# First feed-forward block of a streaming encoder layer: plain products for the first two gated tiles, and the second projection taken product by product per token pair, summed in PSUM

## The chip, the cores and the metric

One NeuronCore of a Trainium2 chip runs one launch of the kernel. The engines in the text are TensorE (PE, matrix products), VectorE (DVE), ScalarE (ACT), GpSimd (POOL) and SyncE (SP), whose queue issues the DMA transfers. The metric is device time in microseconds; less is better.

## The reference

One layer of an encoder: a SwiGLU feed-forward half-step, a mixing step with gated linear attention and stick-breaking attention, and a second SwiGLU half-step, each followed by a layer norm. Tokens are 1024 of a new stream and 64 of a running one, 1088 in all. Only the first half-step is touched:

```python
D_MODEL = 1024; D_FF = 2816; DN_ALPHA = 2 ** 0.25

def swiglu(x, w_in, w_out):
    gate, up = jnp.split(x @ w_in, 2, axis=-1)
    return (jax.nn.silu(gate) * up) @ w_out

def encoder_layer(x, ...):
    h = layer_norm(DN_ALPHA * x + 0.5 * swiglu(x, ffn1_w_in, ffn1_w_out), ln1_g, ln1_b)
    mix, s_new, k_new, v_new = token_mix(h, ...)
    h = layer_norm(DN_ALPHA * h + mix, ln2_g, ln2_b)
    return layer_norm(DN_ALPHA * h + 0.5 * swiglu(h, ffn2_w_in, ffn2_w_out), ln3_g, ln3_b), ...
```

## The kernel before

All data are kept with features on the 128 partitions and tokens along the free dimension. Operands of TensorE are fp32r. To keep fp32 accuracy each operand is split into a high part (`wh`, `xh`: a rounded copy made by ACT) and a low part (`wl`, `xl`: source minus high part, made by POOL or DVE), and one product is three matmuls: wh·xh, wh·xl, wl·xh.

The first half-step has two stages. Stage 1 makes the gate and up projections and the gated product: 22 tiles of 128 hidden features. Stage 2 is the second projection, from 2816 hidden features to 1024. Both use a scheme of seven products in place of eight for 2x2 blocks: input features in two halves, output features in two halves (gate and up in stage 1), tokens in four quarters of 272. Two quarters make a token pair, c = 0 or 1, with 544 tokens. Seven combinations of the input blocks (`xc0` to `xc6`) meet seven combinations of the weight blocks (`weight_forms`, sums `sm`), and the sums of the products are made partly in PSUM, partly by DVE and ACT.

Stage 1. `make_x` builds the seven input forms of each token pair from loaded tiles `big`. The first two tiles (`FIRST`) are taken for token pair 0 first and then for token pair 1, the other 20 for both pairs together: 168 matmuls of 128x272 to a tile, 84 when one pair is done. `gate_up` evicts each product for each pair by itself, 272 columns wide. After every second tile `hidden_forms` makes the seven forms of two hidden tiles and stores them in DRAM, one tensor `d_hc` to a pair of hidden tiles; SP issues those stores.

Stage 2. Six `GROUPS` of hidden pairs (one of 1 pair, five of 2) are run over one after the other; the `xc` slots of stage 1 take the hidden forms that `load_group` reads back, and `load_out` brings the weights in tiles `raw`. The output is a sum in SBUF, `acc` (1024 x 1088), which begins as x (four loads at the line with `acc<-x`). `out_tile` computes the seven products of a group, and DVE adds each of them into `acc` (`onto`) once it is done. The layer norm of tokens 0 to 543 is woven between the last four output tiles of token pair 1. Then the stage's pools close, `split1` splits the normed tokens for the next stage, the first input weights of that stage are loaded (`raw<-w_in`), and `low_rank` and the value projections follow.

The tile framework puts the instructions of each engine in a fixed order when the kernel is built and sets the semaphores; an engine runs its own list in that order. `ahead(gen, n)` makes weight forms n products early.

Of the kernel before, what the change touches and what calls it, by code (L numbers as in the profile page):

```python
# [21 lines left out]
P = 128  # L22
# [12 lines left out]
HW = 272  # L35
NP = NH // 2
GROUPS = [(0, 1), (1, 2), (3, 2), (5, 2), (7, 2), (9, 2)]
# [54 lines left out]
def tile_encoder_layer(  # L92
# [21 lines left out]
    d_hc = [dr.tile([P, 7, 2, 2, HW], F32, name=f"d_hc{p}") for p in range(NP)]  # L114
# [9 lines left out]
    temps = [None, None]  # L124

    def tmp(w, tag):
        pool, bufs = temps
        t = pool.tile([P, 384], F32, name=tag, tag=tag, bufs=bufs[tag])
        return t[:, :w]
# [330 lines left out]

    def weight_forms(A, n, pool, on_pool):


        def form(src, i):
            wh = pool.tile([P, 4, P], F32R, name="wh", tag="wh", bufs=7)[:, :n, :]
            wl = pool.tile([P, 4, P], F32R, name="wl", tag="wl", bufs=7)[:, :n, :]
            nc.scalar.copy(wh, src)  # L467
            eng = nc.gpsimd if i in on_pool else nc.vector
            eng.tensor_tensor(wl, src, f32(wh), op=ALU.subtract)  # L469
            return wh, wl  # L470

        def add(a, b):
            t = pool.tile([P, 4, P], F32, name="sm", tag="sm", bufs=3)[:, :n, :]
            nc.vector.tensor_tensor(t, a, b, op=ALU.add)
            return t

        a11, a12, a21, a22 = A
        yield form(a11, 0)
        yield form(a12, 1)
        s1 = add(a21, a22)  # L480
        s2 = add(a11, s1)
        yield form(s2, 2)
        yield form(s1, 3)
        yield form(add(a11, a21), 4)
        yield form(a22, 5)
        yield form(add(a12, s2), 6)

    def token_forms(B, form, neg, add, sub):

        b11, b12, b21, b22 = B  # L490
        form(0, b11)
        form(1, b21)
        n1 = sub(b11, b12)
        t2 = add(b22, n1)
        neg(2, t2)
        form(3, n1)
        form(4, sub(b22, b12))
        form(5, sub(t2, b21))
        form(6, b22)

    def seven(forms, xs, cs, A, B, evac, want=None):

        n = None
        for i in range(NPROD):
            wh, wl = next(forms)
            bank = A if i in (0, 2, 4, 5) else B(i)
            fresh = i in (0, 1, 3)
            for c in cs:
                x = xs(i, c)
                n = len(x)  # L510
                for k, (xh, xl) in enumerate(x):
                    o = bank[:, c, :HW]
                    kw = dict(skip_group_check=True)
                    nc.tensor.matmul(o, wh[:, k, :], xh, start=(fresh and k == 0), stop=False, **kw)  # L514
                    nc.tensor.matmul(o, wh[:, k, :], xl, start=False, stop=False, **kw)  # L515
                    nc.tensor.matmul(o, wl[:, k, :], xh, start=False, stop=(k == n - 1), **kw)  # L516
            for c in cs:
                evac(i, c, bank[:, c, :HW])
            yield cost(3 * n * len(cs), HW)
# [6 lines left out]
    XF = [xa, xb]  # L526

    def bank_a():
        return pq.tile([P, 2, 512], F32, name="qa", tag="qa")

    def banks_b():
        held = {}

        def b(i):
            if i != 6:
                held[0] = pq.tile([P, 2, 512], F32, name="qb", tag="qb", bufs=2)
            return held[0]

        return b

    def big(dtype=F32):
        return p1.tile([P, 4 * HW], dtype, name="big", tag="big", bufs=6)

    def load_gate_up(j):
        raws = []
        for g in range(2):
            raw = ws.tile([P, 1024], F32, name="raw", tag="raw", bufs=4)
            r0 = (2 * j + g) * P
            nc.sync.dma_start(out=raw, in_=f1_in[r0 : r0 + P, :])
            raws.append(raw.rearrange("p (k m) -> p k m", m=P))  # L550
        g, u = raws
        return [g[:, :4], g[:, 4:], u[:, :4], u[:, 4:]]


    XC = {}

    def load_x(c):
        B = {}
        for jt in ((0, 0), (1, 0), (0, 1), (1, 1)):
            j, t = jt  # L560
            q = big()
            t0 = (2 * c + t) * HW
            nc.sync.dma_start(
                out=q.rearrange("p (k w) -> p k w", w=HW),
                in_=x[j * 512 : (j + 1) * 512, t0 : t0 + HW].rearrange("(k p) w -> p k w", p=P),
            )
            B[jt] = q
            yield q
        yield B

    def make_x(c, B, eng):
        XC[c] = [None] * NPROD

        def out(i):
            t = XF[c].tile([P, 2, 4 * HW], F32R, name=f"xc{i}", tag=f"xc{i}")
            XC[c][i] = t
            return t[:, 0, :], t[:, 1, :]

        def form(i, src):
            h, l = out(i)  # L580
            nc.scalar.copy(h, src)  # L581
            eng.tensor_tensor(l, src, f32(h), op=ALU.subtract)  # L582

        def neg(i, src):
            h, l = out(i)
            nc.scalar.mul(h, src, -1.0)
            nc.vector.scalar_tensor_tensor(l, src, -1.0, f32(h), op0=ALU.mult, op1=ALU.subtract)

        def two(op):
            def f(a, b):  # L590
                t = big()
                eng.tensor_tensor(t, a, b, op=op)
                return t

            return f

        token_forms((B[0, 0], B[0, 1], B[1, 0], B[1, 1]), form, neg, two(ALU.add), two(ALU.subtract))

    def x_of(i, c):
        t = XC[c][i].rearrange("p h (k w) -> p h k w", w=HW)  # L600
        return [(t[:, 0, k, :], t[:, 1, k, :]) for k in range(4)]

    def ev(tag):
        return p1.tile([P, 2, HW], F32, name=tag, tag=tag)

    hid = {}

    def gate_up(j, cs, forms):

        if j not in hid:  # L610
            hid[j] = big().rearrange("p (h c w) -> p h c w", h=2, c=2)
        h = hid[j]
        a, b = bank_a(), banks_b()
        s1, u2, u3, g1, g2, v = (ev(n) for n in ("s1", "u2", "u3", "g1", "g2", "v"))

        def evac(i, c, ps):
            if i == 0:
                nc.scalar.copy(s1[:, c, :], ps)
            elif i == 1:
                nc.vector.tensor_tensor(g1[:, c, :], s1[:, c, :], ps, op=ALU.add)  # L620
                nc.scalar.activation(g1[:, c, :], g1[:, c, :], AF.Silu)
            elif i == 2:
                nc.scalar.copy(u2[:, c, :], ps)
            elif i == 4:
                nc.scalar.copy(u3[:, c, :], ps)
# [5 lines left out]
            elif i == 6:  # L631
# [4 lines left out]
                )  # L636

        return seven(forms, x_of, cs, a, b, evac)

    def hidden_forms(p):  # L640

        lo, hi = hid.pop(2 * p), hid.pop(2 * p + 1)
# [926 lines left out]
```

## Time and profile before

| | |
|---|---|
| median of 3 runs | 3078.06 us (3076.51 to 3080.78) |
| profiled execution, its own time | 3076.39 us |
| span of the profiled execution | 3074.7 us |
| busy share: PE / DVE / ACT / POOL | 95% / 46% / 34% / 33% |
| mean granted TensorE clock | 0.977 |
| mean DMA rate | 100 GB/s |

The span runs from the first to the last instruction; 1.7 us of the time lie around it. The parts of the program that the change touches are the first 930 us or so: stage 1, stage 2, and the passage to the next stage. The engines' busy share over the whole span says little on them; the stretches below do.

### The profile page before, as it was taken

The numbers are of one execution on the slowest core, as the hardware profiler recorded it, in microseconds if no ns is written. First come the engines' busy times: TensorE is split into PE (matmuls) and PEld (weight loads), VectorE is DVE, ScalarE is ACT, GpSimd is POOL, SyncE is SP. The second block draws the span as 40 slices with busy tenths as digits, with TensorE's granted clock in tenths as the row PEclk, the third lists the DMA queues.
The fourth block names the chain that finished last, engine by engine and source line by source line (L and its number), as shares of the span: only waits on it lengthen the run. The fifth ranks groups of instructions, "written<-read, shape, count | busy, mean of one in ns | idle before, by whom it ended". The sixth has DMA issues, their size and how long they took to land.

```text
span 3074.7 us, 47634 instructions
## 1 busy us (share of the span) xinstructions
PE 2908.0 (95%) x19240; PEld 2829.9 (92%) x19240; DVE 1408.5 (46%) x2429; ACT 1038.9 (34%) x2145; POOL 1023.0 (33%) x866
## 2 busy tenths in 40 slices
PE   4999999699869999999999999999899999999997
PEld 4999999599759999999999999999799999999997
DVE  6656555577883354324444443242851211212225
ACT  4444444222465344323333333321553111111115
POOL 7334433222462211122332222332854121222235
PEclk8999999899979999999999999999999999999998
DMA  3334334845153322251335232634432111111123
GB/s 120 128 136 151 144 121 168 345 178 224 54 111 61 55 42 54 52 108 53 85 57 80 51 81 73 191 110 128 155 105 90 48 42 42 49 49 42 42 83 106
DMA packets 210283, 308.44 MB, mean 100 GB/s; under 512 B 12592, under 2 KB 177200, under 8 KB 210064
## 3 DMA queue, kind: packets, MB, share of 16 engines
q1 hardware_dynamic: 196240, 287.58, 32.4%
q10 hardware_dynamic: 13824, 17.83, 1.6%
q8 instruction: 151, 2.47, 0.3%
q14 instruction: 68, 0.56, 0.1%
HBM read 225.77 MB, written 79.59 MB: 99 GB/s over the span
## 4 chain that ended last, share of the span: by engine, by line
PE 83%; DVE 7%; POOL 3%; ACT 2%; issue 2%; DMA 1%; SPq 0%; DVEq 0%; POOLq 0%; ACTq 0%
PE mm L231 11%; PE mm L233 11%; PE mm L232 11%; PE qa L514 4%; PE qa L516 3%; PE qa L515 3%; PE up L232 3%; PE up L231 3%; PE up L233 3%; PE av L1238 2%; PE qb L514 2%; PE qb L515 2%; PE qb L516 2%; PE mm L442 2%; PE mm L444 2%; PE mm L443 2%
## 5 line engine op out<-in xcount | busy, mean ns | idle before, releaser
L182 POOL TENSOR_TENSOR wl<-raw,wh 128x512 fp32r<-128x512 f32 (+1 forms) x366 | 535.5, 1483 | 1188.3 <-ACT wh L181 1176.5
L181 ACT CAST wh<-raw 128x512 fp32r<-128x512 f32 (+1 forms) x366 | 233.3, 667 | 642.5 <-PE mm L232 205.6
L514 PE MATMUL qa<-xc,wh 128*128 128x272 f32 x1056 | 323.7, 306 | 80.5 <-DVE acc L770 20.8
L516 PE MATMUL qa<-xc,wl 128*128 128x272 f32 x1056 | 310.5, 294 | 0.7 <-POOL wl L469 0.7
L515 PE MATMUL qa<-xc,wh 128*128 128x272 f32 x1056 | 309.6, 293 | 0.0
L469 POOL TENSOR_TENSOR wl<-raw,wh 128x512 fp32r<-128x512 f32 (+2 forms) x156 | 164.2, 1056 | 425.6 <-ACT wh L467 374.4
L514 PEld LDWEIGHTS qa<-xc,wh 128*128 128x128 f32 x1056 | 203.8, 193 | 101.4 <-DVE acc L768 24.8
L231 PE MATMUL mm<-X2h,wh 128*128 128x320 f32 (+1 forms) x752 | 242.0, 322 | 5.2 <-DVE g L1397 2.9
L516 PE MATMUL qb<-xc,wl 128*128 128x272 f32 x792 | 231.7, 293 | 12.7 <-POOL wl L469 12.7
L231 PE MATMUL mm<-X0h,wh 128*128 128x384 f32 (+1 forms) x688 | 233.9, 340 | 6.5 <-DVE qs L970 5.8
L233 PE MATMUL mm<-X2h,wl 128*128 128x320 f32 (+1 forms) x752 | 237.6, 316 | 1.9 <-POOL wl L182 1.9
L232 PE MATMUL mm<-X2l,wh 128*128 128x320 f32 (+1 forms) x752 | 237.4, 316 | 0.0
L514 PE MATMUL qb<-xc,wh 128*128 128x272 f32 x792 | 233.5, 295 | 1.1 <-ACT xc L581 0.6
L515 PE MATMUL qb<-xc,wh 128*128 128x272 f32 x792 | 231.4, 292 | 2.8 <-DVE xc L582 2.8
L233 PE MATMUL mm<-X0h,wl 128*128 128x384 f32 (+1 forms) x688 | 230.8, 336 | 1.2 <-POOL wl L182 1.2
L232 PE MATMUL mm<-X0l,wh 128*128 128x384 f32 (+1 forms) x688 | 230.0, 334 | 0.0
L231 PE MATMUL mm<-X1h,wh 128*128 128x384 f32 x624 | 212.9, 341 | 0.0
L233 PE MATMUL mm<-X1h,wl 128*128 128x384 f32 x624 | 208.7, 335 | 0.0
L232 PE MATMUL mm<-X1l,wh 128*128 128x384 f32 x624 | 208.6, 334 | 0.0
L516 PEld LDWEIGHTS qa<-xc,wl 128*128 128x128 f32 x1056 | 204.2, 193 | 1.4 <-POOL wl L469 1.4
L515 PEld LDWEIGHTS qa<-xc,wh 128*128 128x128 f32 x1056 | 204.7, 194 | 0.2 <-DVE xc L582 0.2
L311 DVE SCALAR_TENSOR_TENSOR sg<-sg,up 128x384 f32<-128x384 f32 (+1 forms) x66 | 35.1, 532 | 364.5 <-PE up L233 363.6
(306 smaller groups left out, 7732.2 us busy)
## 6 DMA issues: line engine op xcount, KB each, us to landing
raw<-f_in SPq DMA_DIRECT2D x108, 512.0 KB, 3.6
d_hc<-big SPq DMA_DIRECT2D x77, 544.0 KB, 3.4
xc<-d_hc SPq DMA_DIRECT2D x77, 544.0 KB, 9.4
raw<-w_in SPq DMA_DIRECT2D x70, 512.0 KB, 7.9
raw<-f_out SPq DMA_DIRECT2D x48, 512.0 KB, 3.7
raw<-w_ao SPq DMA_DIRECT2D x16, 512.0 KB, 4.0
raw<-w_bo SPq DMA_DIRECT2D x16, 512.0 KB, 3.8
raw<-w_o SPq DMA_DIRECT2D x16, 512.0 KB, 3.7
```

The lines of the kernel that those rows point to most:

```text
L181: nc.scalar.copy(oh, src)
L182: nc.gpsimd.tensor_tensor(ol, src, f32(oh), op=ALU.subtract)
L231: nc.tensor.matmul(ps[:, :w], wh[:, k, :], xh[:, k, :], start=(k == 0), stop=False)
L232: nc.tensor.matmul(ps[:, :w], wh[:, k, :], xl[:, k, :], start=False, stop=False)
L233: nc.tensor.matmul(ps[:, :w], wl[:, k, :], xh[:, k, :], start=False, stop=(k == KT - 1))
L442: nc.tensor.matmul(ps[:n, :256], a, wh, start=(k == 0), stop=False)
L443: nc.tensor.matmul(ps[:n, :256], b, wh, start=False, stop=False)
L444: nc.tensor.matmul(ps[:n, :256], a, wl, start=False, stop=(k == KT - 1))
L469: eng.tensor_tensor(wl, src, f32(wh), op=ALU.subtract)
L514: nc.tensor.matmul(o, wh[:, k, :], xh, start=(fresh and k == 0), stop=False, **kw)
L515: nc.tensor.matmul(o, wh[:, k, :], xl, start=False, stop=False, **kw)
L516: nc.tensor.matmul(o, wl[:, k, :], xh, start=False, stop=(k == n - 1), **kw)
```

## The change

Four things change; what is computed stays.

1. Tiles 0 and 1 are computed by eight plain products per tile and token pair (`plain_gate_up`, 96 matmuls) from the unsummed quarters of x. The seven forms of x are built by `combine_x`, called after the second and the last of these calls.
2. Tiles 2 to 21 keep their seven products. Evictions take both token pairs at once, 544 columns wide. `hidden_forms` becomes a generator that is advanced by one step after each product; its stores are issued from ACT's queue, each one a step after its form is made, and the DRAM tensors are now one per product (`d_hc[i]`, all 11 pairs, per token pair) and not one per hidden pair.
3. Stage 2 runs over token pairs, and in each over the seven products (`ORDER`), with all 2816 features summed in PSUM before an eviction. The four weight blocks lie in SBUF (`a00`, `a01`, `a11`, `a10`, 704 KB per quarter of a block, 2.9 MB per block); their sums are made in place on DVE (`plus`), and three blocks are loaded again during token pair 1. The hidden forms of a product are loaded in one transfer of 128 x 5984 values (3.06 MB) into one of two slots (`hf0`, `hf1`). Products that share an output keep their PSUM bank (`a0` to `a3`).
4. The layer norm of tokens 0 to 543 is woven in two parts of 272 between the products of token pair 1, and `split1` gives every other low part to DVE.

The core of the diff:

```diff
-GROUPS = [(0, 1), (1, 2), (3, 2), (5, 2), (7, 2), (9, 2)]
+KH = [(0, 4), (4, 4), (8, 3)]
-    d_hc = [dr.tile([P, 7, 2, 2, HW], F32, name=f"d_hc{p}") for p in range(NP)]
+    d_hc = [dr.tile([P, 2, NP, 2 * HW], F32, name=f"d_hc{i}") for i in range(7)]
+    ORDER = {0: (0, 1, 5, 3, 2, 4, 6), 1: (2, 3, 4, 6, 0, 1, 5)}
...
+    def plain_gate_up(j, c, forms):
+        h = hidden(j)
...
+        for g in range(2):
+            bank = pq.tile([P, 2, 512], F32, name="qb", tag="qb", bufs=2)
+            w = forms[2 * g : 2 * g + 2]
+            for t in range(2):
+                for jj in range(2):
+                    mm4(bank[:, t, :HW], w[jj], *xs(jj, t), start=(jj == 0), stop=(jj == 1))
+            if g == 0:
+                g1 = ev("g1")
+                nc.scalar.activation(g1, bank[:, :, :HW], AF.Silu)
...
     def hidden_forms(p):
...
+        def flush():
+            while send:
+                i, st = send.pop()
+                nc.scalar.dma_start(out=d_hc[i][:, :, p, :], in_=f32(st).rearrange("p (c e) -> p c e", c=2))
+        def out(i, src, neg=False):
+            flush()
+            st = p1.tile([P, 4 * HW], F32R, name="st", tag="st", bufs=3)
...
-    for c in range(2):
-        for j in FIRST:
...
-            drain(gate_up(j, (c,), forms))
+    plain_gate_up(0, 0, forms)
...
+    plain_gate_up(0, 1, forms)
+    forms = [wform(t, 4, nc.gpsimd) for t in load_gate_up(1)]
+    plain_gate_up(1, 0, forms)
+    combine_x(0, nc.vector)
+    plain_gate_up(1, 1, forms)
+    combine_x(1, nc.gpsimd)
...
     for j in js:
-        drain(gate_up(j, (0, 1), forms))
+        for _ in gate_up(j, forms):
+            next(pend, None)
...
+    load_hf(0, 0, most)
+    load_block((0, 0))
+    load_hf(0, 1, most)
+    load_block((0, 1))
+    load_hf(0, 0, rest)
+    load_hf(0, 1, rest)
+    load_acc(0)
+    load_block((1, 1))
+    load_block((1, 0))
...
+                    yield wform(blk(FROM[i]), kn, nc.vector if n % 5 in (1, 3) else nc.gpsimd)
+                    if c == 0:
+                        if i == 5:
+                            plus((1, 1), (1, 0))
...
+            for s, i in enumerate(ORDER[c]):
+                if (c, s) != (0, 0) and (c, s) != (1, 6):
+                    load_hf(*((c, s + 1) if s < 6 else (1, 0)), whole)
...
+                    for k in range(kn):
+                        nc.tensor.matmul(o, wh[:, k, :], xh, start=(kk == 0 and not acc_on), stop=False, **kw)
+                        nc.tensor.matmul(o, wh[:, k, :], xl, start=False, stop=False, **kw)
+                        nc.tensor.matmul(o, wl[:, k, :], xh, start=False, stop=(kk == NP - 1), **kw)
...
+                        elif i == 4:
+                            onto(m + 1, 0, o, sub)
+                            onto(m + 1, 1, o, sub)
...
-    weave(chain(norm1(0, 384, nothing, (6.0, 7.0)), norm1(384, 160, nothing, (4.0, 4.0))), fill)
+    weave(chain(norm1(0, HW, nothing, (20.0, 9.0)), norm1(HW, HW, nothing, (9.0, 9.0))), fill)
...
-    for m in range(KT):
-        split1(0, 384, m, nc.gpsimd)
+            split1(t0, w, m, nc.gpsimd if m % 2 else nc.vector)
```

The order of DVE's first instructions, before: sums of weight blocks (`sm`) and of x blocks (`big`) stand between the low parts of the first input forms (L582).

```order
L582 TENSOR_TENSOR xc_116<-big,xc_116 128x1088
L474 TENSOR_TENSOR sm<-raw 128x512
L474 TENSOR_TENSOR sm<-raw,sm 128x512
L474 TENSOR_TENSOR sm<-raw 128x512
L582 TENSOR_TENSOR xc_119<-big,xc_119 128x1088
L592 TENSOR_TENSOR big<-big 128x1088
L474 TENSOR_TENSOR sm<-raw,sm 128x512
L592 TENSOR_TENSOR big<-big 128x1088 x2
L582 TENSOR_TENSOR xc_129<-big,xc_129 128x1088
```

The same place now (L545 is the low part of a quarter of x; `b_115` is that of the quarter that has no slot of its own; L574 to L577 are halves of the combinations).

```order
L545 TENSOR_TENSOR xc_100<-xc_110,xc_100 128x1088
L545 TENSOR_TENSOR xc_101<-xc_111,xc_101 128x1088
L574 TENSOR_TENSOR g_487<-xc_110,xc_111 128x544
L545 TENSOR_TENSOR b_115<-xc_111,b_114 128x1088
L575 TENSOR_TENSOR ht<-xc_110,xc_111 128x544
L545 TENSOR_TENSOR xc_104<-xc_110,xc_104 128x1088
L576 TENSOR_TENSOR ht<-xc_110,g_487 128x544
```

The four low parts of the first token pair now stand within the first six rows of DVE's list, with two half-width combinations between them; the sums of weight blocks are gone from this place.

SP's list between the stages, before (`d_hc_78` holds the last hidden pair's forms; `xc` are loads for stage 2).

```order
L657 DMA d_hc_78<-big 128x1088 x2
L744 DMA xc_5932<-d_hc_68 128x1088
L657 DMA d_hc_78<-big 128x1088 x5
L744 DMA xc_5940<-d_hc_70 128x1088
L744 DMA xc_5943<-d_hc_69 128x1088
L733 DMA acc<-x 128x2x1088 x4
```

SP's list at that place now (`hf_5613`, `hf_5619`, `hf_5841` are the hidden forms of the first, second and third product; `a_5610`, `a_5611`, `a_5612`, `a_5621` the four weight blocks; the stores are in ACT's list).

```order
L774 DMA hf_5613<-d_hc_68 128x5440
L779 DMA a_5610<-f_out 128x1408 x4
L774 DMA hf_5619<-d_hc_69 128x5440
L779 DMA a_5611<-f_out 128x1408 x4
L774 DMA hf_5613<-d_hc_68 128x544
L774 DMA hf_5619<-d_hc_69 128x544
L783 DMA acc_5605<-x 128x2x544 x4
L779 DMA a_5612<-f_out 128x1408 x4
L779 DMA a_5621<-f_out 128x1408 x4
L774 DMA hf_5841<-d_hc_73 128x5984
```

Before, the small loads for stage 2 stood in SP's list among the last stores; now 3.06 MB slots and whole blocks follow in a row, and the load for the third product is behind all four blocks and the first half of `acc`.

ACT's list at that place now (L686 and L681 make the high parts of the last hidden forms, L674 stores them, L472 is the first cast of a weight of stage 2):

```order
L686 CAST st<-ht 128x2x272
L681 ACTIVATE st<-ht 128x2x272
L686 CAST st<-ht 128x2x272
L674 DMA d_hc_73<-st 256x1x544
L674 DMA d_hc_70<-st 256x1x544
L674 DMA d_hc_72<-st 256x1x544
L686 CAST st<-hd 128x2x272
L472 CAST wh<-a_5610 128x512
L674 DMA d_hc_74<-st 256x1x544
```

The stores of the last hidden pair and its last casts now stand ahead of the first weight cast of stage 2 in one list; before, ACT's list held no DMA here.

## Rows read from the trace of the kernel before

**Rows 1.** Stretches of the span: busy us (instructions), granted clock, DMA share, GB/s

```profile
0.00:100.00 100.00, 57.32 (x322) 52.65 (x323) 69.35 (x62) 43.16 (x69) 64.68 (x41) 0.85 0.36 117
106.00:540.00 434.00, 424.04 (x3298) 416.92 (x3297) 250.98 (x402) 184.91 (x405) 168.29 (x119) 1.00 0.39 144
547.00:566.00 19.00, 0.13 (x1) 0.13 (x1) 4.95 (x8) 2.98 (x6) 5.26 (x4) 0.56 0.93 353
566.00:780.00 214.00, 200.68 (x1489) 193.03 (x1490) 155.01 (x411) 50.14 (x135) 54.50 (x77) 0.98 0.60 226
780.00:851.00 71.00, 56.18 (x351) 50.59 (x349) 63.54 (x153) 32.59 (x78) 31.76 (x41) 0.89 0.21 64
851.00:930.00 79.00, 52.47 (x291) 43.67 (x290) 60.31 (x97) 50.48 (x109) 51.29 (x49) 0.79 0.51 111
```

**Rows 2.** Waits in 0 to 106 us: total us, times, longest

```profile
PE qb L516 <- POOL wl L469: 12.7, 2, 6.5
PE qa L514 <- ACT u L623: 12.5, 3, 9.9
...
PE qa L514 <- ACT wh L467: 6.7, 1, 6.7
```

**Rows 3.** First eviction of tiles 2 to 21, both token pairs (stage 1)

```profile
L618 ACT COPY s<-qa x40: 372/380/390, 108.5 to 527.1; 128x272 f32<-128x272 f32 x40
```

**Rows 4.** Timeline of PE at the start of stage 2: start us, duration

```profile
565.87 0.59 PE L514 MATMUL qa<-xc,wh 128*128 128x272 f32 x1 [19.08 <-DVE acc L770]
...
566.49 0.43 PE L516 MATMUL qa<-xc,wl 128*128 128x272 f32 x1
566.72 0.43 PE L514 MATMUL qa<-xc,wh 128*128 128x272 f32 x1
...
570.16 0.29 PE L515 MATMUL qb<-xc,wh 128*128 128x272 f32 x1
570.29 0.29 PE L516 MATMUL qb<-xc,wl 128*128 128x272 f32 x1
```

**Rows 5.** Groups of 0 to 106 us, by shape: busy us, mean ns

```profile
L582 DVE TENSOR_TENSOR xc<-big,xc 128x1088 fp32r<-128x1088 f32 x6 | 8.8, 1460 | 5.9 <-ACT xc L581 5.9
```

**Rows 6.** Groups of 106 to 545 us, by shape

```profile
L469 POOL TENSOR_TENSOR wl<-raw,wh 128x512 fp32r<-128x512 f32 x57 | 78.9, 1383 | 246.6 <-ACT wh L467 246.6
...
L656 POOL TENSOR_TENSOR big<-ht,big 128x544 fp32r<-128x544 f32 x30 | 47.1, 1584 | 4.8 <-ACT big L655 4.5
...
L474 DVE TENSOR_TENSOR sm<-raw,sm 128x512 f32<-128x512 f32 x37 | 25.5, 688 | 0.7
```

**Rows 7.** Waits of PE in 106 to 545 us

```profile
PE qa L514 <- ACT s L618: 9.3, 10, 1.0
```

**Rows 8.** Waits in 545 to 851 us

```profile
PE qa L514 <- DVE acc L770: 20.8, 3, 19.1
...
PE qa L514 <- DVE acc L768: 14.6, 19, 3.3
DVE acc L770 <- DMA acc<-x: 12.8, 1, 12.8
```

**Rows 9.** Groups of 566 to 851 us, by shape

```profile
L768 DVE TENSOR_TENSOR acc<-acc,qa 128x272 f32<-128x272 f32 x168 | 67.0, 433 | 46.1 <-PE qa L516 45.8
```

**Rows 10.** The stretch in which most DMA issues were in flight

```profile
560.00:580.00 20.00, 13.43 (x78) 11.91 (x78) 12.37 (x38) 3.35 (x13) 2.93 (x7) 0.76 1.02 412
```

**Rows 11.** DMA issues of 540 to 640 us: KB each, us to landing

```profile
d_hc<-big SPq DMA_DIRECT2D x7, 544.0 KB, 3.2
```

**Rows 12.** PE's timeline after the end of stage 2

```profile
863.14 1.09 PE L242 MATMUL st<-s,ones 128*128 128x224 f32 x2 [11.82 <-DVE s L251]
865.52 0.53 PE L877 MATMUL mm<-X0h,wlr 128*32 128x384 f32 x1 [1.30 <-DVE wlr L154]
```

**Rows 13.** SP's timeline there

```profile
846.42 1.81 SPq L169 DMA_DIRECT2D raw<-w_in  x2
```

**Rows 14.** DVE's timeline there

```profile
853.24 6.29 DVE L272 SCALAR_TENSOR_TENSOR acc<-acc,vc,r 128x160 f32<-128x160 f32 x8
```

More of the change, by code (lines that the diff above doesn't have):

```diff
@@ L459, in tile_encoder_layer @@
     NPROD = 7
[L461 to L519, printed above, removed]
+    ORDER = {0: (0, 1, 5, 3, 2, 4, 6), 1: (2, 3, 4, 6, 0, 1, 5)}
     ws, ws_close = open_pool("ws")
@@ L713, in ahead, with load_in @@
             pull()
-    def all_forms(tiles, n_of, load, on_pool):
-        for t in tiles:
-            yield from weight_forms(load(t), n_of(t), ws, on_pool)
-    js = range(len(FIRST), NH)
-    forms = ahead(all_forms(js, lambda j: 4, load_gate_up, (0, 1, 5)), 5)
+    def load_in(j, g):
+        raw = ws.tile([P, 1024], F32, name="raw", tag="raw", bufs=3)
+        r0 = (2 * j + g) * P
+        nc.sync.dma_start(out=raw, in_=f1_in[r0 : r0 + P, :])
+        v = raw.rearrange("p (k m) -> p k m", m=P)
+        return [v[:, :4], v[:, 4:]]
@@ new lines, in ev, with hidden, mm4 @@
+    def ev(tag):
+        return p1.tile([P, 2, HW], F32, name=tag, tag=tag)
+    hid = {}
+    def hidden(j):
+        if j not in hid:
+            hid[j] = p1.tile([P, 4 * HW], F32, name="hd", tag="hd", bufs=3).rearrange(
+                "p (t c w) -> p t c w", t=2, c=2
+            )
+        return hid[j]
+    def mm4(o, w, xh, xl, start, stop):
+        kw = dict(skip_group_check=True)
+        wh, wl = w
+        for k in range(4):
+            s = slice(k * HW, (k + 1) * HW)
+            nc.tensor.matmul(o, wh[:, k, :], xh[:, s], start=(start and k == 0), stop=False, **kw)
+            nc.tensor.matmul(o, wh[:, k, :], xl[:, s], start=False, stop=False, **kw)
+            nc.tensor.matmul(o, wl[:, k, :], xh[:, s], start=False, stop=(stop and k == 3), **kw)
@@ L794, in tile_encoder_layer @@
-    last = len(GROUPS) - 1
-    steps = [(g, mp, (0, 1)) for g in range(last) for mp in range(4)]
-    steps += [(last, mp, (c,)) for c in range(2) for mp in range(4)]
-    oforms = ahead(
-        all_forms(steps, lambda t: GROUPS[t[0]][1], lambda t: load_out(t[0], t[1]), (0, 1, 3, 5)), 5
-    )
-    groups = {0: load_group(0)}
-    def outs(steps):
-        for g, mp, cs in steps:
-            if mp == 0 and g + 1 <= last and g + 1 not in groups:
-                groups[g + 1] = load_group(g + 1)
-            yield from out_tile(g, mp, cs, groups[g], oforms)
@@ L808, in tile_encoder_layer, with load_hf @@
-    drain(outs(steps[:-4]))
+    TW[0] = HW
+    A = {}
+    for ij in ((0, 0), (0, 1), (1, 1)):
+        A[ij] = f2.tile([P, 4, NP * P], F32, name="a%d%d" % ij, tag="a%d%d" % ij)
+    hf = {}
+    def load_hf(c, s, part):
+        i = ORDER[c][s]
+        if (c, s) not in hf:
+            par = (7 * c + s) % 2
+            hf[c, s] = f2.tile([P, NP, 2, HW], F32R, name=f"hf{par}", tag=f"hf{par}")
+        t = hf[c, s].rearrange("p k h w -> p k (h w)")
+        nc.sync.dma_start(out=f32(t[:, part, :]), in_=d_hc[i][:, c, part, :])
@@ new lines, in load_block, with load_acc @@
+    def load_block(ij):
+        for mp in range(4):
+            r0 = ((2 * ij[0] + ij[1]) * 4 + mp) * P
+            nc.sync.dma_start(out=A[ij][:, mp, :], in_=f1_out[r0 : r0 + P, :])
+    def load_acc(c):
+        for m in range(0, KT, 2):
+            nc.sync.dma_start(
+                out=acc[c][:, m : m + 2, :],
+                in_=x[m * P : (m + 2) * P, c * 2 * HW : (c + 1) * 2 * HW].rearrange("(k p) w -> p k w", p=P),
+            )
+    most, rest, whole = slice(0, NP - 1), slice(NP - 1, NP), slice(0, NP)
```

485 lines of the change are left out of this document (282 added, 203 removed).

## The prediction

> **What bounds the kernel now.** I read the table of stretches first [rows 1], because a busy share of 95% over the span hides where PE stands still. In stage 1's long stretch, 106 to 540 us, PE is busy 424 of 434 us: there only fewer or faster matmuls count. Around it the picture is another: in the first 100 us PE works 57.3 us, between 547 and 566 us nothing, and from 780 to 851 us 56.2 of 71 us at a granted clock of 0.89, while DVE is busy 63.5 us. The waits say why. At the start PE waits for POOL's low parts (12.7 us in two waits), for an eviction on ACT (12.5) and for a cast (6.7, the wait ahead of the very first matmul) [rows 2]: the seven-product start needs sums of x and of weights before it can go on. Between the stages PE stands still for 19.08 us before the matmul at 565.87 [rows 4]; it waits for DVE's first addition into the output sum, and that waited 12.8 us for the load of x into this sum [rows 8]. In stage 2 PE waits another 14.6 us in 19 waits for such additions [rows 8]. Stage 2's last matmul is over at 863.14 − 11.82 = 851.3 us [rows 12].
>
> The price of a matmul: 570.29 − 570.16 = 0.126 us from start to start (0.125 to 0.13 in the rows around) at the higher of TensorE's two clock levels (2.4 GHz), 566.72 − 566.49 = 0.23 us at the lower one (1.2 GHz), to which PE had fallen in the 19 us without work; it was back some 4 us later [rows 4].
>
> **Start.** Tile 2's first eviction begins at 108.5 [rows 3]; it follows 24 matmuls of 0.126 us, so tile 2 starts at about 105.5 us. Now the first two tiles take 4 x 96 = 384 matmuls, 48 more than the 4 x 84 of before (6.0 us dearer), but they need only the plain quarters of x. 384 x 0.126 = 48.4 us. The first matmul of before is at 6.7 us [rows 2]; two loads and one cast still stand ahead of it, so I take 7.2. The first 30 or so run at the lower level (+3 us): the four low parts at 1.46 us each [rows 5] and two half-width combinations between them in DVE's list come at about the rate at which PE then uses them (12 matmuls to each quarter: 2.7 us cold, 1.5 warm). For later stalls, such as token pair 1's last low part behind the gated product in DVE's list, I take 2.5 us. The combinations themselves cost PE nothing: they are some 20 us of DVE and POOL beside 48 us of matmuls; without that cover they would cost what the waits at the start cost now. Tile 2 starts at 7.2 + 48.4 + 3 + 2.5 = 61 us (58 to 68): **44.5 us gained**.
>
> **Rest of stage 1.** Twenty tiles from 105.5 to 546.8 (565.87 − 19.08) are 22.06 us each; 168 x 0.126 makes 21.2. Of the 0.9 us between, 9.3/20 = 0.47 is the wait for the first eviction, 382 ns a half, ten times in 20 tiles [rows 7]. One eviction of 544 columns is one instruction where two were, but it starts after the second token pair only and ends later. What is new in ACT's list are seven DMA issues per hidden pair, each of which waits for a low part on POOL (1.58 us [rows 6]). They stand a step later than the cast, and POOL is busy 168 of 434 us [rows 1], so most should find it done. Bounds: no loss left (21.2) and as before (22.06). I take 21.65, the middle: 20 x 21.65 = 433 us, **8 us gained**; stage 1 ends at 494.
>
> **Between the stages.** The first load of stage 2 now needs slots that the last matmuls of stage 1 still read; it is issued some 3 us before their end. 2.8 MB of forms and 2.9 MB of weights come at up to 412 GB/s [rows 10], 13.8 us, and ACT's list has the last hidden pair's casts and stores ahead of the first weight cast; a store lands 3.2 us after its issue [rows 11], its form needs a cast and a low part of 1.6 us before that. First matmul about 12 us after stage 1's end, not 19.08: **7 us gained** (0 to 12).
>
> **Stage 2.** 7 products x 4 output tiles x 11 hidden pairs x 3 x 2 token pairs = 1848 matmuls, as before: 232.8 us at 0.126. Before, from 565.87 to 851.3, it took 285.4, so 52.6 us were lost to additions, restarts and the woven norm. Now DVE adds only finished sums, 80 additions of 0.43 us [rows 9] where 7 x 4 x 6 groups x 2 pairs = 336 were, and PE need not wait for a bank in turn. In their place stand 168 weight splits, 128x512 or 128x384, three in five on POOL: about 100 x 1.38 = 139 us [rows 6] in 250, and 48 block sums on DVE at 0.69 us [rows 6], 33 us. Both engines have room, so these I cost at nothing; if POOL lost a third of its rate it would just reach PE's.
>
> What is late next is the third product. By SP's order its forms follow the second slot, three blocks and half of the output sum: 2.8 + 2.9 + 0.6 + 4.5 + 2.9 + 2.9 + 3.1 = 19.5 MB, which at 412 GB/s [rows 10] take 47.4 us from the second slot's issue. That issue waits, by the queue's semaphores, for stores of stage 1's last forms, and comes about 12 to 14 us after stage 1's end. So the forms land 61 us after it. PE, which starts at 12 and needs 2 x 16.6 us for two products and 2 us for the slow restart, is there at 47.5: a stall of **13.5 us**, and a second slow restart, 2 us. The DMA share was 1.02 where 412 GB/s were moved, so this rate is a ceiling here. The Trainium skill, page "DMA: Bandwidth & Descriptors", section "Where 436 GB/s comes from", holds that between HBM and SBUF the HBM side binds at about 358 GB/s; the trace of before moved 412, against that; by the page's figure the stall would be an estimated 20 us, and the total some 7 us more.
>
> Later slots are 3.06 MB each, 7.5 us at that rate and some 2 us more, behind 16.6 us of matmuls: hidden. If they came no faster than one transfer alone, 544 KB in 3.2 us [rows 11], that is 174 GB/s, they would take 18 us, 1.5 us too long for each of some 12 products, and the second half of the output sum another 10 or so on top: 28 us in all. The layer norm of tokens 0 to 543 stands beside 116 us of matmuls of token pair 1, where before it filled the 71 us in which PE was busy 56.
>
> Stage 2: 232.8 + 2 + 13.5 + 2 + 2 for single waits = 252.3 against 285.4: **33 us gained**.
>
> **Passage.** PE waited 11.82 us for a norm whose chain began with eight DVE instructions of 6.29 us in all [rows 12, 14]. That part is now done earlier, and POOL shares its low parts with DVE. Against it: the input weights of the next stage, issued at 846.42 and so 5 us before the end [rows 13], now wait for the last matmul, and land some 6 to 9 us after it. Before, PE was at work again 11.8 us after the end, and had the low-rank weights at 14.2 (865.52). I take 3 us gained (−4 to +7).
>
> **Sum.** 44.5 + 8 + 7 + 33 + 3 = 95.5 us off the profiled execution's own 3076.4 us: 2980.9. That execution lies 1.7 us under the median of the runs, so I forecast **2982 us**.
>
> **The rivals.**
> *Better cover.* Stage 1 at 21.2 us a tile (−9), a stall of 5 us in place of 13.5 and the passage at its best (−4): 2960. For it: the order leaves 9 to 14 matmuls of the next tile between the two products that need the same bank. Against: the rate of [rows 10] is already the highest. Chance 0.13.
> *Late slots.* The large loads come at the rate of a lone transfer, and stage 1 stays at 22.06: +28 and +8, 3018. For it: the stretch 566 to 780 moved 226 GB/s only [rows 1]. Against: its share was 0.60, so more was to be had. Chance 0.20.
> *ACT blocked by its own stores.* ACT's list is in order; a store that waits for POOL holds back the eviction behind it, and PE waits for the bank. There are 77 stores. The change is lost when each costs PE 95.5/77 = 1.24 us; POOL's low part with one split ahead of it is 1.58 + 1.38 = 2.96 us [rows 6]. Were all of that lost each time, 77 x 2.96 = 228 us, or 3210. Against: the store stands a step of about 3 us behind its cast. From 1.24 us up it decides; at 1.6 the time is 2982 + 77 x 1.6 = 3105. Chance 0.09.
> *Nothing.* A blocking of 0.75 us per store (58 us) and the late slots (36 us) together cancel the gain: 3076. Chance 0.03.
>
> **How the numbers follow.** The forecast case, 2966 to 2998, has 0.55: start ±4, stage 1 ±7, boundary and stall ±7, passage ±4, partly cancelling. With the better cover at 2955 and the late slots up to 3028 the range, 2955 to 3028, holds eight in ten; out of it stay the tail of late slots, the blocked ACT and the lost gain. A difference of 0.2% (6 us) is about what can be told from no change here: faster 0.88, same 0.03, slower 0.09.
>
> **What would show it.** Right, if in the new profile tile 2 begins near 61 us, evictions follow each other at about 21.6 us, PE stands still about 12 us between the stages and once more, for 10 to 20 us, ahead of the third product with SP's load as the releaser, and stage 2's end lies near 760. Wrong, if ACT's evictions wait for POOL behind stores, if PE waits for hidden forms in every product, if PE has a second long wait at the start, or if the wait after stage 2 grows beyond 16 us because weights land late.

## The result

The changed kernel takes 2994.6 us (median of 4 runs, 2993.6 to 2997.5) where the kernel before took 3077.9 beside it: a ratio of 0.973 (95% interval 0.9713 to 0.9747). Run a second time, beside later experiments, it gave 2994.0 and 0.9727 (0.9713 to 0.9741). The forecast was 2982 in a range of 2955 to 3028.

The stretches of the changed kernel's span, in the columns of [rows 1] (busy us of PE, weight loads, DVE, ACT, POOL; granted clock, DMA share, GB/s):

```profile
64.00:490.00 426.00, 424.95 (x3353) 422.81 (x3351) 263.89 (x302) 180.68 (x305) 176.12 (x120) 1.00 0.39 139
490.00:512.50 22.50, 0.00 (x0) 0.00 (x0) 3.95 (x6) 3.58 (x6) 3.71 (x4) 0.57 0.93 338
512.50:570.00 57.50, 46.95 (x331) 45.94 (x332) 33.20 (x50) 19.21 (x35) 28.42 (x22) 0.87 1.01 404
570.00:760.00 190.00, 184.37 (x1431) 182.74 (x1430) 115.26 (x195) 88.41 (x165) 105.71 (x86) 0.98 0.57 220
```

And the points on PE's timeline that bound the steps (start us, duration, wait ahead of it with its releaser):

```profile
7.26 0.59 PE L606 MATMUL qb<-xc,wh 128*128 128x272 f32 x1 [7.26 <-ACT xc L544]
...
27.75 0.39 PE L607 MATMUL qb<-b,wh 128*128 128x272 f32 x1 [1.97 <-DVE b L545]
...
62.91 0.29 PE L606 MATMUL qa<-xc,wh 128*128 128x272 f32 x1
...
512.74 0.60 PE L876 MATMUL a<-hf,wh 128*128 128x272 f32 x1 [23.09 <-ACT wh L472]
...
558.95 0.57 PE L876 MATMUL b<-hf,wh 128*128 128x272 f32 x1 [8.85 <-DVE a L820]
...
578.89 0.39 PE L878 MATMUL b<-hf,wl 128*128 128x272 f32 x1 [1.38 <-DVE wl L473]
...
704.26 0.40 PE L878 MATMUL b<-hf,wl 128*128 128x272 f32 x1 [1.77 <-DVE wl L473]
...
782.97 1.12 PE L243 MATMUL st<-s,ones 128*128 128x224 f32 x2 [10.53 <-DVE s L252]
```

62.91 is the first matmul of tile 2; stage 1 ends at 512.74 − 23.09 = 489.65, stage 2 at 782.97 − 10.53 = 772.44. For the kernel before, the working put tile 2 at 105.5 us, 24 matmuls ahead of its first eviction [rows 3]. That eviction came late, and PE's timeline of the kernel before has the tile's first matmul earlier:

```profile
102.75 0.29 PE L514 MATMUL qa<-xc,wh 128*128 128x272 f32 x1
```

So the old start took less, and the 20 old tiles more, than the working has. Against the working, with the first column read anew:

| step | before | forecast | measured | gained: forecast / measured |
|---|---|---|---|---|
| tile 2 begins at | 102.75 (working: 105.5) | 61 | 62.9 | 44.5 / 39.8 |
| 20 tiles of stage 1 | 22.20 each (working: 22.06) | 21.65 | 21.34 | 8 / 17.3 |
| PE still between the stages | 19.08 | 12 | 23.09 | 7 / −4.0 |
| stage 2 | 285.4 | 252.3 | 259.7 | 33 / 25.7 |
| from there to the span's end | 2223.4 | 2220.4 | 2219.9 | 3 / 3.5 |
| sum | | | | 95.5 / 82.4 |

Where [rows 1] had PE busy 424.0 of 434 us in stage 1, it is now 424.95 of 426. Where it had waited at the start for low parts, evictions and casts [rows 2], two waits of more than 0.3 us are left after the first matmul, 0.73 and 1.97 us, both for DVE's low parts. The 53 us that stage 2 lost before are 27 now; by the starts of the matmuls between 512 and 772 us, 17 of them are waits and 7.5 are 75 matmuls at the lower clock level.

### The profile page after: what moved, and what is told of

The parts are those of the page before. It is cut to its first block, busy times and chain, and to the rows that moved or that the text cites. A ratio compares the mean times of both kernels' runs of the same rounds, so it can differ in the third digit from the quotient of the medians.

```text
span 2992.3 us, 46718 instructions
## 1 busy us (share of the span) xinstructions
PE 2879.9 (96%) x19288; PEld 2821.5 (94%) x19288; DVE 1322.2 (44%) x1983; ACT 1041.9 (35%) x1991; POOL 1032.3 (34%) x830
## 4 chain that ended last, share of the span: by engine, by line
PE 71%; DVE 6%; ACT 2%; issue 1%; POOL 1%; DMA 1%; DVEq 0%; POOLq 0%; ACTq 0%
PE mm L232 11%; PE mm L234 11%; PE mm L233 11%; PE up L232 3%; PE up L233 3%; PE up L234 3%; PE av L1338 3%; PE mm L443 2%; PE mm L445 2%; PE mm L444 2%; PE up L364 1%; PE up L365 1%; PE mm L364 1%; PE up L363 1%; PE mm L365 1%
## 5 line engine op out<-in xcount | busy, mean ns | idle before, releaser
L606 PE MATMUL qa<-xc,wh 128*128 128x272 f32 x640 | 186.2, 291 | 0.7 <-ACT u L656 0.7
L608 PE MATMUL qa<-xc,wl 128*128 128x272 f32 x640 | 185.1, 289 | 0.0
L607 PE MATMUL qa<-xc,wh 128*128 128x272 f32 x640 | 184.6, 288 | 0.0
L606 PE MATMUL qb<-xc,wh 128*128 128x272 f32 x576 | 168.1, 292 | 7.4 <-ACT xc L544 7.3
L607 PE MATMUL qb<-xc,wh 128*128 128x272 f32 x576 | 167.7, 291 | 0.7 <-DVE xc L545 0.7
L608 PE MATMUL qb<-xc,wl 128*128 128x272 f32 x576 | 167.9, 291 | 0.0
L473 POOL TENSOR_TENSOR wl<-a,wh 128x512 fp32r<-128x512 f32 (+1 forms) x100 | 128.7, 1300 | 107.8 <-ACT wh L472 107.1
L232 PEld LDWEIGHTS mm<-X2h,wh 128*128 128x128 f32 x752 | 142.4, 189 | 8.2 <-ACT wh L182 3.8
L234 PEld LDWEIGHTS mm<-X2h,wl 128*128 128x128 f32 x752 | 142.3, 189 | 2.4 <-POOL wl L183 2.4
L472 ACT CAST wh<-a 128x512 fp32r<-128x512 f32 (+1 forms) x168 | 96.5, 584 | 134.5 <-PE b L877 73.0
```

The lines of the kernel that those rows point to most:

```text
L232: nc.tensor.matmul(ps[:, :w], wh[:, k, :], xh[:, k, :], start=(k == 0), stop=False)
L234: nc.tensor.matmul(ps[:, :w], wl[:, k, :], xh[:, k, :], start=False, stop=(k == KT - 1))
L606: nc.tensor.matmul(o, wh[:, k, :], xh[:, s], start=(start and k == 0), stop=False, **kw)
L607: nc.tensor.matmul(o, wh[:, k, :], xl[:, s], start=False, stop=False, **kw)
L608: nc.tensor.matmul(o, wl[:, k, :], xh[:, s], start=False, stop=(stop and k == 3), **kw)
```

## The experiments

Each ratio is to the kernel before, run beside it. Times are medians of 4 or 5 runs; points of the profile are of one execution each.

**The start put back.** Tiles 0 and 1 as seven products, pair by pair:

```diff
-    plain_gate_up(0, 0, forms)
-    ...
+    for c in range(2):
+        ...
+        combine_x(c, (nc.vector, nc.gpsimd)[c])
+        for j in range(2):
+            drain(gate_up(j, in_forms(load_gate_up(j)), (c,)))
```

> The changed kernel with tiles 0 and 1 put back to seven products, token pair by token pair, each pair after all of its combinations of x. Theory A (the start's gain is the plain products, which need no sums of x or of weights): tile 2's first matmul moves from 62.9 us to about 105, the total rises by about 42 us to 3037. Theory B (the start is set by the loads of x and the splits, which both versions have): it moves by less than 10 us and the total stays under 3005.

3032.5 us, ratio 0.984 (0.9823 to 0.9858). The long waits are back; PE's timeline of this kernel:

```profile
11.65 0.60 PE L601 MATMUL qa<-xc,wh 128*128 128x272 f32 x1 [11.65 <-ACT wh L472]
...
32.16 0.59 PE L601 MATMUL qa<-xc,wh 128*128 128x272 f32 x1 [14.10 <-ACT wh L472]
...
70.82 0.59 PE L601 MATMUL qb<-xc,wh 128*128 128x272 f32 x1 [8.85 <-ACT xc L539]
```

Tile 2 begins at 98.2 us, not the 105 of theory A, and stage 1 ends at 546.82 − 23.13 = 523.7 us, 34 us later. That is theory A in the main: with seven products PE waits again for the sums. But the edit also puts the loads and casts of weights behind those of x, and its first matmul comes at 11.65 and not at 7.26; 4.4 of the 34 us are this order. How the rest divides between the sums and the order of the lists was not taken apart.

**Stage 1: forms in one go, and evictions per pair.** The first edit drains `hidden_forms` after every second tile; the second evicts each token pair by itself.

```diff
-    pend = hidden_forms(0)
+    drain(hidden_forms(0))
...
-        for _ in gate_up(j, forms):
-            next(pend, None)
+        drain(gate_up(j, forms))
         if j % 2:
-            drain(pend)
-            pend = hidden_forms(j // 2)
+            drain(hidden_forms(j // 2))
-    drain(pend)
```

> The changed kernel with the seven hidden forms of two tiles made in one go after every second tile, as before, and not one step per product. Theory A (stage 1's gain of 0.73 us per tile comes from spreading the forms, because ACT ran their casts between the evictions PE waits for): PE waits about 1 us per pair of tiles again and the total rises by some 14 us to 3009. Theory B (it comes from one eviction of 544 columns in place of two of 272): no change, within 4 us of 2995.

```diff
-            ps = bank[:, :, :HW]
-            if i == 0:
-                nc.scalar.copy(s1, ps)
+            for c in range(2):
+                ps = bank[:, c, :HW]
+                if i == 0:
+                    nc.scalar.copy(s1[:, c], ps)
...
```

> The changed kernel with every eviction of stage 1 taken for each token pair by itself, 272 columns, as before; the forms stay spread. Theory A (spreading of the forms made the gain): no change, within 4 us of 2995. Theory B (the joint eviction made it: a half can no longer be pushed behind other casts in ACT's list): tiles go back to about 22.06 us and the total to about 3009.

> The changed kernel with both of stage 1's edits undone: the hidden forms in one go after every second tile, and evictions per token pair. Theory A (the burst of forms in ACT's list is what PE waits for, and the joint eviction of 544 columns only makes the wait behind a burst longer: 5.1 us per pair of tiles with it): without it the loss per pair is that of the kernel before, 1.9 us, and the total is some 15 us above the changed kernel. Theory B (a burst costs 5 us per pair with either eviction): 45 to 50 us above.

Forms in one go: 3045.0, 0.9891 (0.9876 to 0.9906), 50 us slower than the changed kernel, not 14. Evictions per pair: 2990.9, 0.9715 (0.9701 to 0.973), not to be told from 0.973; stage 1 ends at 489.9, as in the changed kernel. Both: 3031.5, 0.9855 (0.9841 to 0.9869), 37.5 us above the changed kernel's 2994.0 beside it, between what the two theories said. So the joint eviction earns nothing that these runs can tell, and the spreading does, but by another road than I thought. ACT's timeline of the first of the three, and PE's beside it:

```profile
405.45 4.00 ACTq L674 DMA_DIRECT2D d_hc<-st  x3
409.49 0.64 ACT L686 CAST st<-hd 128x544 fp32r<-128x544 f32 x1 [4.47 <-DVE sm L481]
...
410.60 0.59 ACT L654 COPY u<-qa 128x544 f32<-128x544 f32 x1
```

```profile
363.50 0.39 PE L606 MATMUL qa<-xc,wh 128*128 128x272 f32 x1 [3.20 <-ACT u L654]
...
411.24 0.39 PE L606 MATMUL qa<-xc,wh 128*128 128x272 f32 x1 [3.18 <-ACT u L654]
```

and POOL's, whose low parts the stores send:

```profile
405.38 1.73 POOL L473 TENSOR_TENSOR wl<-raw,wh 128x512 fp32r<-128x512 f32 x1
407.07 1.82 POOL L687 TENSOR_TENSOR st<-ht,st 128x544 fp32r<-128x544 f32 x1
```

Three stores stand in a row in ACT's list, the last one until POOL's low part ends at 408.89, and ACT computes nothing for 4.5 us; behind them is the eviction that PE waits for. The period is 47.7 us per pair of tiles against 42.7: 3.2 us of wait, and matmuls at 0.23 us for a time after it. This is the rival of ACT blocked by its own stores. In the changed kernel the spreading keeps it away.

In the kernel before, SP issued the stores, and the forms in one go cost less. ACT's timeline there, and PE's next wait:

```profile
194.96 0.38 ACT L618 COPY s<-qa 128x272 f32<-128x272 f32 x1
195.53 0.66 ACT L650 ACTIVATE big<-ht 128x544 fp32r<-128x544 f32 x1 [0.19 <-DVE ht L664]
196.09 0.63 ACT L655 CAST big<-ht 128x544 fp32r<-128x544 f32 x1
197.31 0.64 ACT L655 CAST big<-ht 128x544 fp32r<-128x544 f32 x1 [0.58 <-issue]
197.86 0.38 ACT L618 COPY s<-qa 128x272 f32<-128x272 f32 x1
```

```profile
198.29 0.39 PE L514 MATMUL qa<-xc,wh 128*128 128x272 f32 x1 [0.92 <-ACT s L618]
```

Three casts of hidden forms stand between the two halves of the eviction, and PE waits for the second half. These are the 9.3 us of [rows 7]; in the changed kernel one wait of 0.7 us is left. The other half of stage 1's gain of 17.3 us lies in smaller gaps and was not traced to a cause. The spreading with the stores left to SP was not run, so whether they had to move to ACT's list is not shown.

**The norm's cover.** Begun with some 50 us of products left, not 116; and, in the kernel before, the norm of tokens 0 to 543 left out:

```diff
-    weave(chain(norm1(0, HW, nothing, (20.0, 9.0)), norm1(HW, HW, nothing, (9.0, 9.0))), fill)
+    drain(fill, 66.0)
+    weave(chain(norm1(0, HW, nothing, (6.0, 5.0)), norm1(HW, HW, nothing, (6.0, 5.0))), fill)
```

```diff
-        yield from layer_norm(w, View(t0, w), V_LN1G, V_LN1B, emit, waits)
+        if t0 >= 544:
+            yield from layer_norm(w, View(t0, w), V_LN1G, V_LN1B, emit, waits)
+        else:
+            yield 1.0
```

> The changed kernel with the layer norm of tokens 0 to 543 begun only when some 50 us of token pair 1's products are left, in place of 116. Theory A (of stage 2's gain of 25.7 us nearly all is the norm's cover: before, 71 us at the end of stage 2 held 44 us of matmuls, after they hold none to spare): PE waits between the last products and the total rises by 10 to 27 us, to 3005 to 3022. Theory B (the gain is that DVE no longer adds every product into the output sum): the norm fits behind 50 us as well, and the total stays within 4 us of 2995.

> The kernel before without the layer norm of tokens 0 to 543 (left out; those tokens go on as they are). Theory A (the norm among the last products, on a DVE that also adds every product, is what the last 71 us of stage 2 lose): stage 2's end moves from 851 to 823 to 830 us. Theory B (the additions alone keep DVE behind): it stays above 840 us.

The late norm: 3001.6, 0.9745 (0.9731 to 0.976), which overlaps that of the changed kernel and lies between the two theories; its span is 7.3 us longer, and PE's timeline has two new waits for sums of the norm:

```profile
746.63 1.25 PE L243 MATMUL st<-s,ones 128*128 128x272 f32 x2 [3.87 <-DVE s L252]
...
759.24 0.73 PE L243 MATMUL st<-s,ones 128*128 128x272 f32 x2 [1.20 <-DVE s L267]
```

The kernel before without that norm: 3050.2, 0.9916 (0.9902 to 0.993). Its stage 2 ends at 834.6 us:

```profile
841.33 1.11 PE L242 MATMUL st<-s,ones 128*128 128x224 f32 x2 [6.71 <-DVE s L251]
```

That is 16.7 us before 851.3 and between the two theories, 4.6 us past A's; 1.2 of the 16.7 are an earlier start of stage 2 in this execution (564.66 and not 565.87). So the norm among additions was at most 15.5 us, three fifths of stage 2's gain of 25.7; at most, because leaving it out takes its own matmuls away too. In the changed kernel 50 us of products cover it nearly, once DVE has few additions beside it. How the other 10 us divide between additions and the rest was not taken apart.

**The third product.** The fourth weight block behind the third product's forms; the first product's casts on DVE; both:

```diff
     load_block((1, 1))
-    load_block((1, 0))
...
+                if (c, s) == (0, 1):
+                    load_block((1, 0))
```

```diff
-    def wform(src, n, eng):
+    def wform(src, n, eng, cast=nc.scalar.copy):
...
-        nc.scalar.copy(wh, src)
+        cast(wh, src)
...
-                    yield wform(blk(FROM[i]), kn, nc.vector if n % 5 in (1, 3) else nc.gpsimd)
+                    early = (c, s) == (0, 0)
+                    yield wform(
+                        blk(FROM[i]), kn,
+                        nc.vector if n % 5 in (1, 3) and not early else nc.gpsimd,
+                        nc.vector.tensor_copy if early else nc.scalar.copy,
+                    )
```

> The changed kernel with the load of the fourth weight block (2.9 MB) moved behind that of the third product's hidden forms in SP's list. Theory A (PE's 8.85 us ahead of the third product end with those forms' landing, DMA being the bound there): they land 2.9 MB / 0.41 = 7 us earlier, the wait shrinks to about 2 us, the total falls by about 7 us to 2988. Theory B (the profile's releaser is right: PE waits for DVE, which runs 24 block sums in a row): the sums need this block and come later, so the wait stays or grows, the total is 2995 or more.

> The changed kernel with the casts of the first product of stage 2 on DVE (all its low parts on POOL), so that they do not stand behind the last hidden forms and stores in ACT's list. Theory A (ACT's list held up the first matmul, and DMA sets when the third product starts): the wait of 23.1 us between the stages shrinks to 12 to 15 us, but the wait ahead of the third product grows by as much, and the total stays within 3 us of 2995. Theory B (the 23 us on PE's path are lost for good): the total falls by 8 to 11 us to about 2985. Theory C (the weights and forms themselves land that late): the first wait stays at 22 us or more.

> Both edits of the two runs before the last: fourth block behind the third product's forms, and the first product's casts on DVE. Theory A (DMA sets the third product's start, ACT's list the first one's): the gain is that of the moved block alone, 7 us, plus at most 2: 2986 to 2988, and PE's wait ahead of the third product is then 8 to 12 us again. Theory B (both waits are separate losses on PE's path): 7 + 9 = 16 us, 2979.

Block moved: 2990.5, 0.9725 (0.9712 to 0.9738). PE's timeline, and its waits from 553 to 610 us:

```profile
553.07 0.56 PE L877 MATMUL b<-hf,wh 128*128 128x272 f32 x1 [2.62 <-DMA hf<-d_hc]
```

```profile
PE b L879 <- DVE wl L473: 4.8, 3, 2.2
PE a L879 <- DVE wl L473: 2.9, 2, 1.7
```

The third product starts 5.9 us earlier, near the 7 us of 2.9 MB, as theory A has it, and the total still does not move clear of the changed kernel: low parts on DVE are late for 7.7 us in five waits, where the changed kernel has 3.2 us in two. The gain is given back.

Casts on DVE: 2997.8, 0.9747 (0.9733 to 0.976):

```profile
502.44 0.57 PE L881 MATMUL a<-hf,wh 128*128 128x272 f32 x1 [12.94 <-DVE wh L472]
514.45 0.60 PE L883 MATMUL a<-hf,wl 128*128 128x272 f32 x1 [11.21 <-POOL wl L473]
...
558.07 0.56 PE L881 MATMUL b<-hf,wh 128*128 128x272 f32 x1 [7.19 <-DVE a L820]
```

The first matmul came 10 us earlier, so ACT's list did hold it back and theory C falls. But I had put the low parts on POOL, whose list has the last hidden forms ahead of them, and PE stood 11.2 us there. The third product came at 558.07 all the same; since PE was not at it sooner, this run alone does not decide between A and B.

Both edits: 2987.4, 0.9714 (0.9701 to 0.9728), A's number and not B's 2979, and not clear of the changed kernel either. But A's wait of 8 to 12 us ahead of the third product did not come: PE stood 11.09 us for a low part on POOL again, and the forms land at 551.2, just ahead of the third product's first matmul at 551.36. So this run does not decide between A and B either.

What sets the third product's start is shown by the traces side by side. In the changed kernel the load of its forms is issued at 539.50 us and takes 19.3 us to land, at 558.8; PE's matmul is at 558.95. In the run with evictions per pair stage 2's first matmul came 3 us sooner, the wait is 2 us longer, and the releaser is the load:

```profile
557.50 0.57 PE L877 MATMUL b<-hf,wh 128*128 128x272 f32 x1 [10.81 <-DMA hf<-d_hc]
```

There it is issued at 537.21 and lands 20.2 us later, at 557.4. In the three kernels with the moved block or the casts on DVE, and in the next one, the third product's first matmul also stands 0.1 to 0.2 us behind this landing. An earlier first matmul of stage 2 alone would thus have moved the wait to the third product, as theory A of the casts has it.

**Sums of weight blocks on POOL.**

```diff
-                        nc.vector.tensor_tensor(blk(a), blk(a), blk(b), op=ALU.add)
+                        nc.gpsimd.tensor_tensor(blk(a), blk(a), blk(b), op=ALU.add)
```

> The changed kernel with the 48 sums of weight blocks on POOL in place of DVE. Theory A (the sums delay low parts in DVE's list; three waits of 1.4 to 1.8 us and two falls of the clock behind them, some 9 us): those waits on DVE go, POOL, with 0.3 of its time free there, has room, and the total falls by 5 to 9 us to about 2987. Theory B (each sum takes POOL 1.4 us and up, 67 us in all, and then POOL's own low parts are late): PE waits for POOL, the total rises by 5 us or more.

3029.8, 0.9851 (0.9837 to 0.9865): theory B, 35 us above the changed kernel. The sums' durations (min, median, max ns, first and last start), and PE's wait for POOL from 560 to 620 us:

```profile
L820 POOL TENSOR_TENSOR a<-a,a x48: 986/1259/1772, 552.4 to 614.6; 128x512 f32<-128x512 f32 x32, 128x384 f32<-128x384 f32 x16
```

```profile
PE b L878 <- POOL wl L473: 27.5, 6, 13.9
```

All 48 sums run within 62 us, ahead of low parts that are due, and the first of these is 13.9 us late. Its row for the third product is worth a look beside that of the changed kernel:

```profile
558.93 0.57 PE L876 MATMUL b<-hf,wh 128*128 128x272 f32 x1 [8.24 <-DMA hf<-d_hc]
```

With no sums on DVE the wait is the same, at the same place, and the releaser is the load. The "DVE a L820" of the changed kernel's row was not what PE waited for.

**An attempt at a better one.** Evictions per pair, the moved block, and low parts of token pair 0's third and fourth product on POOL alone:

```diff
+... nc.vector if n % 5 in (1, 3) and (c, s) not in ((0, 2), (0, 3)) else nc.gpsimd)
```

> The changed kernel with stage 1's evictions per token pair, the fourth weight block behind the third product's forms, and all low parts of token pair 0's third and fourth product on POOL. Theory A (after the moved block what is left on PE's path there are low parts late on DVE, and the clock that falls behind them): those waits go in the stretch from 555 to 600 us, and the total is 10 to 17 us under the changed kernel beside it. Theory B (POOL cannot make 24 low parts in 33 us: 16 x 1.38 + 8 x 1.0 = 30 us leave it no room): the waits move to POOL and the total is within 5 us of the changed kernel.

> The changed kernel once more, beside the three kernels that follow: all theories expect 0.973 of the kernel before, within 0.0015.

2995.0, 0.9734 (0.972 to 0.9748): nothing gained beside 2994.0. The waits moved again:

```profile
585.58 0.57 PE L878 MATMUL b<-hf,wh 128*128 128x272 f32 x1 [4.33 <-DVE acc L846]
```

The total is theory B's, but neither theory names this: POOL kept up, and an eviction that frees a PSUM bank stands behind the sums in DVE's list just as the low parts did; a later low part on DVE costs PE another 2.82 us. No version here beats the changed kernel clearly.

## Why the prediction held, and where it was off

**Start.** Right: tile 2 at 62.9 (61 forecast), with the stall that was named, a low part of token pair 1 behind the gated product on DVE, 1.97 us of the 2.5 allowed. The 3 us for matmuls at the lower clock level came true in sum, 31 of them and 3.1 us, but in part by luck: about half ran not at the start but behind that stall, where the granted clock was 0.51 from 29.0 to 32.5 us. The gain is 39.8 and not 44.5 us mainly because the old start was read 2.75 us too late.

**Stage 1.** Right in sign, too small: 21.34 and not 21.65 us a tile. I gave the gain to no single cause; half of it is the wait for an eviction whose halves the hidden forms' casts held apart, which the spreading ends; the cause of the other half stays open. The joint eviction, which I had in the balance, earns nothing that can be told. The rival of ACT's blocked stores was described rightly and did not come, for the reason given against it: a store stands a step behind its cast. Without the step it costs 50 us.

**Between the stages.** This is the step that failed: "First matmul about 12 us after stage 1's end". It was 23.09. I took 3.2 us for a store's landing [rows 11], from stores that had loads of 544 KB beside them. ACT's and SP's timelines of the changed kernel:

```profile
500.88 0.66 ACT L681 ACTIVATE st<-ht 128x544 fp32r<-128x544 f32 x1 [5.75 <-DMA d_hc<-st]
503.16 0.64 ACT L686 CAST st<-ht 128x544 fp32r<-128x544 f32 x1 [1.62 <-DMA d_hc<-st]
...
511.52 0.64 ACT L686 CAST st<-hd 128x544 fp32r<-128x544 f32 x1 [7.72 <-DMA d_hc<-st]
512.08 0.61 ACT L472 CAST wh<-a 128x512 fp32r<-128x512 f32 x1
```

```profile
486.66 0.33 SPq L774 DMA_DIRECT2D hf<-d_hc  x1
487.04 16.38 SPq L779 DMA_DIRECT2D a<-f_out  x4
511.57 0.33 SPq L774 DMA_DIRECT2D hf<-d_hc  x1
```

The last hidden forms have three buffers `st`; a form waits until an older store has landed, and the stores, now among 2.8 MB and 2.9 MB loads, took 8.3 to 12.3 us (median 10.2); in stage 1, at a DMA share of 0.39, the same stores had taken 3.1 us (median of 70). So ACT waits 15 us in three pieces, and its first weight cast stands behind. The second slot's load, which waits for these stores, was issued 21.9 us after stage 1's end, not 12 to 14.

**Third product.** The mechanism is shown by the moved block, by the run with the sums on POOL and by the landings. The stall was 8.85 and not 13.5 us, because PE came 13 us later than I had it; the forms landed 69 us after stage 1's end, not 61. From the slot's issue it was 47.4 us as forecast, but by luck: I had put half of the output sum at 4.5 MB where it is 2.2, so the list holds 17.3 MB; 405 GB/s over 47.4 us are 19.2 MB, so some 2 MB from outside the list moved in that time too, the last stores among them. The rate was 404 GB/s at a share of 1.01 over 57.5 us. The Trainium skill, page "DMA: Bandwidth & Descriptors", section "Where 436 GB/s comes from", has the HBM side bind at about 358 GB/s; this trace does not agree. The rival of late slots did not come: after the third product no wait of PE in stage 2 is for hidden forms.

**Stage 2's engines.** "Both engines have room, so these I cost at nothing" was wrong in place, not in sum. DVE's timeline:

```profile
550.50 14.49 DVE L820 TENSOR_TENSOR a<-a,a 128x512 f32<-128x512 f32 x24
```

While PE waits for forms, DVE has 24 of the sums done in a row, and it is busy 39.8 of the 40 us from 550 to 590; low parts between the other sums come late, two waits of 1.38 and 1.79 us and a fall of the clock behind the second. The third wait of this size, 1.77 us at 704.26, stands behind the woven norm in the same list:

```profile
697.96 1.46 DVE L257 TENSOR_TENSOR acc<-acc,st 128x272 f32<-128x272 f32 x4
...
703.53 1.72 DVE L473 TENSOR_TENSOR wl<-a,wh 128x512 fp32r<-128x512 f32 x2
```

Beside the stall stage 2 lost 18 us where 6 were forecast; of the 27 us in all the stall took 8.85. Over the stage both engines do have room; POOL was busy 137 us, near the 139 of the working. The aside that POOL would just reach PE's rate if it lost a third of its own is off: 139 of 250 us leave it room to lose over two fifths.

**Norm and passage.** Right in the main: the norm is hidden but for the wait at 704.26, the passage gained 3.5 us.

**The sum.** The total lies 13 us above the forecast, still in the forecast case of 2966 to 2998, and that is partly luck: stage 1 gave 9 us more than forecast, while the start (5), the stretch between the stages (11) and stage 2 (7) gave less.

## What to carry to other kernels

A DMA issue in the list of a computing engine holds that engine until the data are ready (three stores in a row held ACT for 4.5 us): it needs a step between the data's last writer and the issue, and the order of the whole list around it is part of the edit. When small transfers share the DMA engines with bulk loads, price their landing inside the bulk, not from a stretch with small loads, and look at what has few buffers behind them. A stage that starts by filling SBUF is paced by the bytes ahead of its first missing operand, so order loads by first use, and expect the next engine in line to take back a part.

## What the runs showed of the hardware

A wait of 1.79 us was followed by a fall of the clock, and not at once. PE's timeline of the changed kernel:

```profile
587.71 0.39 PE L878 MATMUL b<-hf,wl 128*128 128x272 f32 x1 [1.79 <-DVE wl L473]
...
588.44 0.29 PE L877 MATMUL b<-hf,wh 128*128 128x272 f32 x1
588.56 0.29 PE L878 MATMUL b<-hf,wl 128*128 128x272 f32 x1
...
589.47 0.43 PE L877 MATMUL b<-hf,wh 128*128 128x272 f32 x1
589.70 0.43 PE L878 MATMUL b<-hf,wl 128*128 128x272 f32 x1
```

The matmuls behind the wait start every 0.125 us, at the higher of the two levels (2.4 GHz), and from 589.0 to 592.2 every 0.23 us, at the lower (1.2 GHz): 14 matmuls, 1.4 us more, nearly doubling the wait's price. The wait of 1.77 us at 704.26 had the same sequel, that of 1.38 us at 578.89 had none.

The length of the wait alone does not decide it. The changed kernel with the late norm has the same wait in the same place, and its granted clock stays at 1.00 behind it (columns of [rows 1]):

```profile
587.68 0.40 PE L878 MATMUL b<-hf,wl 128*128 128x272 f32 x1 [1.79 <-DVE wl L473]
```

```profile
588.80:592.20 3.40, 3.40 (x30) 3.40 (x29) 3.40 (x5) 1.59 (x3) 1.57 (x1) 1.00 0.02 7
```

So some 1.4 us behind such a wait come and go from one execution to the next, and differences of a few microseconds between these kernels can hold them.
